# A hybrid decoder trunk on one core: residual kept with tokens on partitions, down projection as seven half-block products of sums

## The chip, the core and the metric

The kernel runs on one core of one Trainium2 chip. The core has a matrix engine (TensorE, "PE" in the profile), a vector engine (DVE), a scalar engine (ACT), GpSimd (POOL), a queue of transfers (SP) and two memories on chip, one of which (PSUM) takes the products. The metric is the device time of one execution in microseconds (us), as the median of several runs.

## The reference

Two layers, each with a token mixer of four head groups (spatial gating, retention, forgetting attention, latent attention) and a squared-ReLU channel MLP, over 512 tokens of width 1024 in float32. The parts that the change touches, cut to what matters:

```
for l in range(DEPTH):                      # DEPTH = 2
    h = rms_norm(x, g_mix_norm[l])
    y = ...four groups from h @ w_in[l], each normalised...
    x = x + y @ w_out[l]
    h = rms_norm(x, g_ffn_norm[l])
    x = x + square(relu(h @ w_up[l])) @ w_down[l]     # D_FF = 4096
return rms_norm(x, g_final)
```

## The kernel before

**Products.** Each float32 operand is split into a rounded high part and a low remainder. A product of 128 rows is three matrix instructions (`three`: high by high, high by low, low by high), so that a product over 1024 rows by 512 columns is 24 of them. A unit of weights (`Unit`, 128 x 1024, 0.5 MB) is fetched by SP into a tile `raw`; ACT casts it into `wh`, DVE subtracts into `wl`.

**Residual.** `xT` holds x with the features on partitions: 8 tiles of 128 features by 512 tokens. In the output projection and in the MLP the weights are the operand that is loaded into the matrix engine, and 512 tokens stream past them (`feat_tile`). Each result of 128 x 512 is added to its tile of `xT` by DVE. `Norm.feed` then scales it by the gain, splits it, squares it on ACT and sums the squares over the eight tiles on POOL and DVE. `tok_rsqrt` sums over partitions with a matrix of ones (`onesr`), and `bcast_tok` brings the factor 1/rms back to all partitions, again with products by ones.

**MLP.** D_FF is taken in four quarters of 1024. For each quarter eight up tiles are made (each from its own unit of weights), evacuated by DVE (ReLU times the factor `rbc`), squared on ACT and split; then eight down tiles of 24 instructions each are added to `xT`. The last quarter of the last layer makes its down tiles for 256 tokens at a time, and normalises and stores one half while the other is computed.

**Order.** All instructions are recorded with what they read and write. A list scheduler (`_Order.schedule`) then writes a fixed order for each engine, from costs and latencies in a table, with the numbers of buffers as limits: `u` (128 x 512, 46 buffers), `wh` and `wl` (6 each), `raw` (3), `quad` (3), and the eight banks of PSUM in tags `acc` 2, `s` 3, `t` 2, `pv` 1. On the chip each engine works through its order and waits where an operand is not there. All engine instructions are issued from one line of the recorder, L202, so rows of the profile are told apart by tile names, out<-in, the input that streams first and the one that is loaded second.

Of the kernel before, what the change touches and what calls it, by code (L numbers as in the profile page):

```python
# [11 lines left out]
F32 = mybir.dt.float32  # L12
# [21 lines left out]
NU = 46  # L34
NW = 6

# per-layer parameter columns
# [7 lines left out]
# shape-only constant columns  # L45
# [8 lines left out]
class _Tile:  # L54
    """A tile of a pool, taken from it when its first writer is emitted."""

    def __init__(self, od, pool, tag, bufs, shape, dtype, psum):
        self.pool, self.tag, self.bufs, self.shape, self.dtype, self.psum = pool, tag, bufs, shape, dtype, psum
        self.name = f"{tag}_{len(od.tiles)}"
        self.real = None  # L60
        self.left = 0
        self.seq = od.tag_n.setdefault(tag, [0, bufs, []])
        self.no = len(self.seq[2])
        self.seq[2].append(self)
        self.writes, self.reads = [], []
        self.held = False
        od.tiles.append(self)
# [11 lines left out]
class _View:  # L79
    """A part of a tile: the steps that lead to it, and what it covers."""  # L80
# [78 lines left out]
class _Op:  # L159
    __slots__ = ("eng", "call", "cost", "lat", "succ", "npred", "ready", "tiles", "news", "prio", "no", "start", "unit", "alt", "table")  # L160


class _Order:
    """Records the kernel's instructions with what they read and write, then issues them in the order of a list
    scheduling: per engine the most urgent instruction whose operands and buffers should be there by then."""
# [40 lines left out]
    def cost(self, eng, fn, out, ins, k):  # L206
        n = int(np.prod(out.shape[1:])) if isinstance(out, _View) else 0
        ps = any(v.tile.psum for v in ins)
        if eng == "pe":
# [6 lines left out]
            return max(n / 2.4 + 2.5, 105.0 if a.dtype == BF16 else 110.0)  # L216
# [15 lines left out]
    def record(self, eng, fn, args, kw):  # L232
# [31 lines left out]
        o.tiles, o.news = [], []  # L264
        for v, wr in [(x, False) for x in ins] + [(x, True) for x in outs]:
# [8 lines left out]
            if t not in o.tiles:  # L274
                o.tiles.append(t)
                t.left += 1
                if not t.writes:
                    o.news.append(t)
# [12 lines left out]
    def schedule(self):  # L291
# [22 lines left out]
        while ev:  # L314
# [9 lines left out]
            for o in cand[e]:  # L324
# [8 lines left out]
                for x in o.news:  # L333
# [24 lines left out]
            for x in o.news:  # L358
# [40 lines left out]
RESERVE = {"u": 10}  # L399
# [4 lines left out]
def hybrid_kernel(ctx: ExitStack, tc: tile.TileContext, xT_d, par_d, sgu_d, con_d, con2_d, wg2_d, win_d, wmla_d, wout_d, wup_d, wdn_d, out_d):  # L404
# [22 lines left out]

    def quad():
# [5 lines left out]
    class prio:  # L434
        """urgency of what is recorded inside: its place in the program, moved forward by `ahead`"""
# [20 lines left out]
    # ---------------------------------------------------------------- tensor engine  # L456
    def mm(out, a, b, start, stop):
        PE.matmul(out, a, b, start=start, stop=stop)
# [4 lines left out]
    def three(ps, ah, al, bh, bl, first, last):  # L463
        mm(ps, ah, bh, first, False)
        mm(ps, ah, bl, False, False)
        mm(ps, al, bh, False, last)

    # ---------------------------------------------------------------- weights
# [8 lines left out]
    class Unit:  # L477
        def __init__(self, src, n=1024, nsplit=None, spare=False, first=None):
# [4 lines left out]
            self.raw = mk(wpool, "raw", 3, (P, 1024))  # L483
            for c in ((0, n),) if first is None else ((0, first), (first, n)):
                Q.dma_start(self.raw[:, c[0]:c[1]], src[:, c[0]:c[1]])
            self.spare = spare
            if spare:
                self.h, self.l = (u(F32R), u(F32R)), (u(F32R), u(F32R))
                for i in range(2):
                    split(self.h[i], self.l[i], self.raw[:, i * T:(i + 1) * T])  # L490
            else:
                self.h = mk(wpool, "wh", NW, (P, 1024), F32R)
                self.l = mk(wpool, "wl", NW, (P, 1024), F32R)
                for c in ((0, k),) if first is None else ((0, first), (first, k)):
                    cs = slice(*c)
                    (od.copy if first else S.copy)(self.h[:, cs], self.raw[:, cs])
                    V.tensor_tensor(self.l[:, cs], self.raw[:, cs], self.h[:, cs].bitcast(F32), op=ALU.subtract)
            od.unit = None

        def part(self, t, k):  # L500
            return t[k // 4][:, chunk(k % 4)] if self.spare else t[:, chunk(k)]

        def hi(self, k):
            return self.part(self.h, k)

        def lo(self, k):
            return self.part(self.l, k)
# [14 lines left out]
    # ---------------------------------------------------------------- constants  # L522
    xT = cst("xT", (P, KD, T))
    par = cst("par", (P, DEPTH * NPV + KD))
# [4 lines left out]
    Q.dma_start(xT[:, 0], xT_d[:, 0])  # L529
    g2w = [Unit(wg2_d[0, 0], 2 * NG2, first=NG2)]  # L530
    Q.dma_start(xT[:, 1], xT_d[:, 1])
    Q.dma_start(xT[:, 2:4], xT_d[:, 2:4])
    g2w += weights(lambda i: wg2_d[0, i + 1], 1, 2 * NG2)
    Q.dma_start(xT[:, 4:6], xT_d[:, 4:6])
    g2w += weights(lambda i: wg2_d[0, i + 2], 1, 2 * NG2)
    Q.dma_start(xT[:, 6:8], xT_d[:, 6:8])
# [22 lines left out]
    # while the first operands are on their way: the scalar engine's table, and the tensor engine's clock  # L559
# [7 lines left out]
    # ---------------------------------------------------------------- helpers  # L567
# [6 lines left out]
    def split_gain(src, g):  # L574
        h, lo = u(F32R), u(F32R)
# [4 lines left out]
    def tok_rsqrt(acc, n, eps):  # L580
        """per-token (n**-1 * sum_p acc[p, tok] + eps) ** -0.5, tokens on partitions"""
# [13 lines left out]
    def bcast_tok(r):  # L595
        """r[tok, c] -> PSUM [any partition, tok]"""
# [13 lines left out]
    class Norm:  # L610
        """split of x * gain, and the root mean square of x per token"""

        def __init__(self, g, sq_eng=None):
            self.g, self.sq_eng = g, sq_eng
# [3 lines left out]
        def feed(self, k, split=True):  # L618
            xk = xT[:, k]
            if split:  # L620
                self.h[k], self.l[k] = split_gain(xk, self.g[:, k:k + 1])
# [4 lines left out]
            if self.sq_eng is None:  # L626
                S.activation(sq, xk, AF.Square)
            else:
                self.sq_eng.tensor_tensor(sq, xk, xk, op=ALU.mult)
# [3 lines left out]
        def finish(self, bc=True):  # L633
            self.r = tok_rsqrt(self.acc, DM, EPS)
            pb = bcast_tok(self.r)
            if bc:
                self.rbc = u()
                V.tensor_copy(self.rbc, pb)
            else:
                self.rbc = pb  # L640

    def tok_group(us, ncols, nrm, evac, banks):
        """z[tok, ncols] = sum_k, chunks in sets of len(banks)"""
# [14 lines left out]
    def feat_tile(w, ks, evac, m, o0=0, bank="acc"):  # L658
        """output tile of 128 features; ks: hi/lo operand tiles"""
# [42 lines left out]
        # group norm, features on partitions  # L702
# [13 lines left out]
    def tok_to_feat(yt, grp):  # L716
        """yt[c]: [P, 256] token-major, already normalised -> two hi/lo feature tiles with the gain"""
# [8 lines left out]
    def std_heads(src, dst, eps):  # L726
        """dst = standardised src over each head's 64 columns"""
# [491 lines left out]
```

## Time and profile before

| | |
|---|---|
| runs | 1192.19, 1196.79 and 1196.87 us, median 1196.79 |
| profiled execution, first to last instruction | 1192.4 us (the page gives no time for what lies around it) |
| PE busy | 1171.5 us, 98% of the span |
| weight loads into PE | 966.1 us, 81% |
| DVE busy | 685.2 us, 57% |
| ACT busy | 504.8 us, 42% |
| POOL busy | 91.9 us, 8% |
| read from memory | 103.44 MB |

Busy time of an engine is an average over stages: the mixers (about 0 to 245 us and 600 to 830 us) and the MLPs (the rest) have different limits. The chain of waits, followed back from the last instruction, tells which engine sets the end in a stretch.

### The profile page before, as it was taken

What the parts mean: (1) busy time and instruction counts of PE and PEld (TensorE: products, weight loads), DVE (VectorE), ACT (ScalarE), POOL (GpSimd) and SP (SyncE); (2) the same over time, 40 slices, a digit from 0 to 9 for tenths busy, and PEclk for the clock granted to TensorE, in tenths of its full rate; (3) what the DMA queues carried; (4) which work ended last, traced back from release to release, by engine and by line L of the source; (5) the groups of instructions that cost most, each with busy time, mean ns of one, the idle gap of its engine ahead of it and who ended that gap; (6) DMA issues with size and microseconds to landing.
All of it is one profiled execution on the core that took longest, in us unless ns stands there. A gap on an engine that the chain in (4) does not pass through costs nothing.

```text
span 1192.4 us, 14647 instructions
## 1 busy us (share of the span) xinstructions
PE 1171.5 (98%) x5662; PEld 966.1 (81%) x5662; DVE 685.2 (57%) x1299; ACT 504.8 (42%) x865; POOL 91.9 (8%) x100
## 2 busy tenths in 40 slices
PE   8999999999999999999999999999999999999997
PEld 7768788878888888888886778887888888888897
DVE  7985778774344344345469667789643534443533
ACT  6975445444133233134358473455431422322432
POOL 4200012120000000000240000212000000000000
PEclk9999999999999999999999999999999999999999
DMA  7322022223322323232221122132223232323202
GB/s 257 97 71 71 29 96 81 97 71 106 97 98 94 101 92 103 91 104 83 99 84 59 53 67 76 36 124 89 89 89 105 88 107 88 106 88 106 88 19 71
DMA packets 31941, 106.48 MB, mean 89 GB/s; under 512 B 3712, under 2 KB 6400, under 8 KB 31872
## 3 DMA queue, kind: packets, MB, share of 16 engines
q1 hardware_dynamic: 31872, 105.55, 26.8%
q8 instruction: 44, 0.72, 0.3%
q14 instruction: 25, 0.20, 0.1%
HBM read 103.44 MB, written 2.10 MB: 89 GB/s over the span
## 4 chain that ended last, share of the span: by engine, by line
PE 87%; DVE 6%; issue 3%; ACT 2%; DMA 1%; POOL 0%; SPq 0%; POOLq 0%; DVEq 0%; ACTq 0%
PE acc L202 48%; PE s L202 34%; DVE u L202 3%; PE t L202 3%; PE pv L202 2%; ACT u L202 2%; DVE wl L202 1%; DVE xT L202 1%; DMA raw<-win 1%; ACT wh L202 1%; DMA xT<-xT 1%; DVE sm L202 0%; POOL sm L202 0%; SPq L202 0%; DVE state L202 0%
## 5 line engine op out<-in xcount | busy, mean ns | idle before, releaser
L202 PE MATMUL acc<-u,wh 128*128 128x512 f32 (+1 forms) x1376 | 420.6, 385 | 6.9 <-DVE u L202 5.5
L202 ACT CAST wh<-raw 128x1024 fp32r<-128x1024 f32 (+2 forms) x190 | 197.3, 1039 | 519.6 <-PE acc L202 255.8
L202 PE MATMUL s<-u,wh 128*128 128x512 f32 (+1 forms) x1160 | 346.3, 381 | 0.0
L202 PEld LDWEIGHTS acc<-u,wh 128*128 128x128 f32 x1376 | 255.5, 189 | 59.0 <-DVE u L202 6.1
L202 PE MATMUL acc<-u,wl 128*128 128x512 f32 (+1 forms) x688 | 264.8, 385 | 0.0
L202 DVE TENSOR_TENSOR wl<-raw,wh 128x1024 fp32r<-128x1024 f32 (+3 forms) x191 | 231.7, 1214 | 55.2 <-ACT wh L202 54.5
L202 PEld LDWEIGHTS s<-u,wh 128*128 128x128 f32 x1160 | 215.0, 188 | 41.7
L202 PE MATMUL s<-u,wl 128*128 128x512 f32 (+1 forms) x580 | 220.6, 380 | 0.0
L202 PE MATMUL acc<-wh,u 128*128 128x512 f32 (+2 forms) x576 | 169.2, 367 | 0.7 <-ACT wh L202 0.6
L202 PEld LDWEIGHTS acc<-u,wl 128*128 128x128 f32 x688 | 129.7, 189 | 25.6 <-issue 1.1
L202 PEld LDWEIGHTS s<-u,wl 128*128 128x128 f32 x580 | 109.1, 188 | 20.7
L202 PEld LDWEIGHTS acc<-wh,u 128*128 128x128 f32 x576 | 104.3, 189 | 17.8 <-issue 2.0
L202 PE MATMUL acc<-wl,u 128*128 128x512 f32 (+2 forms) x288 | 106.3, 369 | 0.6 <-DVE wl L202 0.6
L202 DVE TENSOR_TENSOR xT<-acc,xT 128x512 f32<-128x512 f32 (+1 forms) x68 | 44.5, 656 | 99.9 <-PE acc L202 99.7
L202 DVE TENSOR_TENSOR u<-u,u 128x512 fp32r<-128x512 f32 (+4 forms) x146 | 94.7, 652 | 11.9 <-ACT u L202 10.9
L202 POOL TENSOR_TENSOR sm<-sm,mhalf 128x4 f32<-128x4 f32 (+3 forms) x38 | 39.5, 1042 | 718.7 <-DVE sm L202 689.6
L202 DVE TENSOR_TENSOR xT<-s,xT 128x512 f32<-128x512 f32 (+1 forms) x52 | 33.7, 648 | 103.6 <-PE s L202 103.5
L202 ACT ACTIVATE u<-u 128x512 f32<-128x512 f32 (+1 forms) x120 | 65.6, 548 | 37.5 <-DVE u L202 36.9
L202 ACT CAST u<-u 128x512 fp32r<-128x512 f32 (+3 forms) x120 | 73.4, 620 | 14.1 <-DVE u L202 11.4
L202 DVE SCALAR_TENSOR_TENSOR u<-acc,u 128x512 f32<-128x512 f32 x36 | 24.8, 690 | 81.8 <-PE acc L202 81.8
L202 DVE SCALAR_TENSOR_TENSOR u<-s,u 128x512 f32<-128x512 f32 x32 | 22.1, 690 | 78.2 <-PE s L202 78.2
L202 POOL TENSOR_TENSOR u<-u,u 128x512 f32<-128x512 f32 x20 | 33.6, 1679 | 373.2 <-ACT u L202 372.5
(111 smaller groups left out, 907.3 us busy)
## 6 DMA issues: line engine op xcount, KB each, us to landing
raw<-wup SPq DMA_DIRECT2D x64, 512.0 KB, 3.3
raw<-wdn SPq DMA_DIRECT2D x64, 512.0 KB, 3.3
raw<-win SPq DMA_DIRECT2D x36, 512.0 KB, 3.4
raw<-wout SPq DMA_DIRECT2D x16, 512.0 KB, 3.3
raw<-wg SPq DMA_DIRECT2D x7, 420.0 KB, 3.2
raw<-wmla SPq DMA_DIRECT2D x4, 512.0 KB, 3.4
xT<-xT SPq DMA_DIRECT2D x3, 512.0 KB, 7.4
outT<-xT SPq DMA_DIRECT2D x6, 256.0 KB, 2.2
```

Source lines behind the costliest of these rows:

```text
L202: getattr(e, fn)(*[g(a) for a in args], **{n: g(a) for n, a in kw.items()})
```

## The change

Four things change together.

**The residual is kept as `xt`, tokens on partitions** (4 tiles of 128 tokens by 1024 features). In the output projection the activations are loaded and 512 columns of weights stream (`out_group`); the result is added to half a tile of `xt`. The mean of squares is accumulated by ACT along the row while it squares (`TokNorm.feed`). For the next products the residual is turned to features on partitions by 32 transposes of 128 x 128 on PE, eight tiles of four, each then scaled and split (`TokNorm.turn`). The factor of the MLP's norm is not applied to the up tiles: its square (`r2`) multiplies the down products when they are added, since ReLU and square let a positive factor through. The last norm needs no products: each token's factor is on its partition.

**The down product of a quarter** (512 tokens x 1024 by 1024 x 1024) is taken as a product of 2 x 2 blocks in the seven-product form: sums and differences of blocks are formed on DVE, four of the activations and four of the weights, then seven products of half blocks (two token tiles, 512 rows, 512 columns: 24 matrix instructions each) are made, and several results are accumulated on in one bank and read by DVE in between (14 additions to `xt` in place of 8). The blocks `2` and `3` of the weights are fetched twice, so a quarter fetches 12 units for its down products in place of 8.

**Alternation.** The up tiles of the next quarter alternate with the seven products: up tile, product, up tile, and so on. The first quarter's eight up tiles stand alone, and so do the last quarter's seven products. ReLU is one instruction on DVE or ACT, the squares are two of 256 columns on either.

**Pools.** `u` 46 to 37 buffers, `wh`/`wl` 6 to 5; `raw` goes, and 10 tiles `big` of 128 x 1024 take fetched weights, the first input, and some tiles of the mixers that lay in `u`. The cost table's figure for a matrix instruction and the limits for reserved buffers change with it.

The diff, cut to its core:

```diff
-NU = 46
-NW = 6
+NU = 37
+NW = 5
+NBIG = 10
...
+    class TokNorm:
...
+        def feed(self, c, hf):
+            S.activation(u(), x2(c, hf), AF.Square, scale=DM ** -0.5, accum_out=self.ss[:, 2 * c + hf:2 * c + hf + 1])
+
+        def turn(self, hf):
+            for k in range(4 * hf, 4 * hf + 4):
+                tp = psum("t")
+                for c in range(NCH):
+                    tr(tp[:, chunk(c)], xt[:, c, k * P:(k + 1) * P])
+                self.h[k], self.l[k] = split_gain(tp, self.g[:, k:k + 1])
...
-        for un in range(4):
-            w = Unit(wout_d[l, un])
-            for i in range(2):
-                feat_tile(w, yD + yC, add, un * 2 + i, i * 512)
...
-        nrm.finish()
...
+        def out_group(units, ks, last=False):
+            for hf in range(2):
+                us = [Unit(wout_d[l, un]) for un in units[hf]]
+                for c in range(NCH):
+                    ps = psum(rot[nout[0] % 5])
...
+                    V.tensor_tensor(x2(c, hf), ps, x2(c, hf), op=ALU.add)
+                    if last:
+                        nrm.feed(c, hf)
+                if last:
+                    nrm.turn(hf)
+
+        out_group([[0, 1], [2, 3]], yD + yC)
+        out_group([[4], [5]], yBT)
+        out_group([[6], [7]], yAT, True)
+        nrm.square()
...
-            def evac_up(t, ps):
-                a = u()
-                V.scalar_tensor_tensor(a, ps, 0.0, nrm.rbc, op0=ALU.max, op1=ALU.mult)
-                S.activation(a, a, AF.Square)
-                hi, lo = u(F32R), u(F32R)
-                split(hi, lo, a)
...
-            for t in range(QBLK):
-                feat_tile(Unit(wup_d[l, qf * QBLK + t]), kin, evac_up, t, bank=rot[t % 5])
...
-            for m in range(KD):
-                feat_tile(Unit(wdn_d[l, qf * KD + m]), act, evac_dn, m, bank=rot[m % 5])
...
+            def product(x, raws, bank, first, done):
+                xs = []
+                for g in range(2):
+                    h, lo = u(F32R), u(F32R)
+                    split(h, lo, X[x, g])
+                    xs.append((h, lo))
+                ws = [Unit(None, raw=raws[g]) for g in range(2)]
+                for p in range(2):
+                    ps = bank(p)
+                    for g in range(2):
+                        for jj in range(2):
+                            o = jj * 256 + p * P
+                            w, cs = ws[g], slice(jj * T, (jj + 1) * T)
+                            with using(w):
+                                three(ps, xs[g][0][:, o:o + P], xs[g][1][:, o:o + P], w.h[:, cs], w.l[:, cs],
+                                      first and g == 0 and jj == 0, g == 1 and jj == 1, skip_group_check=True)
+                    done(p, ps)
...
+            def add(c, hf, ps, done=False):
+                V.scalar_tensor_tensor(x2(c, hf), ps, nrm.r2[:, c:c + 1], x2(c, hf), op0=ALU.mult, op1=ALU.add)
...
+            def p6():
+                fetch(1, 3)
+                for g in range(2):
+                    X["S3", g] = u()
+                diff(Xv("S3"), Xv("11"), Xv("21"))
+                diff(Rv(1), Rv(1), Rv(0))
+                diff(Rv(3), Rv(3), Rv(1))
+                diff(Xv("21"), Xv("21"), Xv("22"), ALU.add)
+                diff(Xv("11"), Xv("21"), Xv("11"))
+                product("11", R[3], bank(B, None), False, lambda p, ps: add(p + 2, 0, ps))
...
+            return [p1, p2, p6, p7, p4, p5, p3]
+
+        for part in ups(0):
+            part()
         for qf in range(nq):
+            a, b = downs(qf), ups(qf + 1) if qf + 1 < nq else []
+            for i in range(max(len(a), len(b))):
+                for part in b[i:i + 1] + a[i:i + 1]:
+                    part()
```

How the instructions stand now, at three places. First PE, in layer 0, where the output projection ends and the MLP begins. Before, the last tile of the output projection (bank `s_2506`) is followed by the first up tile (`acc_2519`, activations `u`, weights `wh_2264` and `wl_2277`):

```order
L202 MATMUL s_2506<-u_2320,wh_2212 128x512
L202 MATMUL s_2506<-u_2330,wh_2212 128x512
L202 MATMUL s_2506<-u_2320,wl_2227 128x512
L202 MATMUL s_2506<-u_2326,wh_2212 128x512
L202 MATMUL s_2506<-u_2337,wh_2212 128x512
L202 MATMUL s_2506<-u_2326,wl_2227 128x512
L202 MATMUL acc_2519<-u_2434,wh_2264 128x512
L202 MATMUL acc_2519<-u_2442,wh_2264 128x512
```

After the change (`s_2534` is the last tile of the output projection, `xt_333` the residual, `con_196` the identity, `s_2559` the first up tile):

```order
L201 MATMUL s_2534<-wh_2332,u_2322 128x512
L201 MATMUL s_2534<-wl_2339,u_2322 128x512
L201 MATMUL s_2534<-wh_2332,u_2330 128x512
L201 MATMUL t_2548<-con_196,xt_333 128x128 x3
L201 MATMUL t_2555<-con_196,xt_333 128x128 x3
L201 MATMUL s_2559<-u_2488,wh_2343 128x512
L201 MATMUL s_2559<-u_2502,wh_2343 128x512
L201 MATMUL t_2548<-con_196,xt_333 128x128
L201 MATMUL t_2555<-con_196,xt_333 128x128
L201 MATMUL s_2559<-u_2488,wl_2360 128x512
L201 MATMUL s_2559<-u_2494,wh_2343 128x512
L201 MATMUL s_2559<-u_2510,wh_2343 128x512
```

The transposes stand between the last output tile and the first up tile, mixed with that tile's first products, which take features turned earlier.

Second DVE, in the last quarter of layer 0's MLP. Before, between two additions to `xT` there are a subtraction for a unit of weights (`wl`) and the split for the next norm:

```order
L202 TENSOR_TENSOR xT_80<-acc_4546,xT_80 128x512
L202 TENSOR_TENSOR wl_4594<-raw_4491,wh_4582 128x1024
L202 SCALAR_TENSOR_TENSOR u_4603<-xT_80,par_72,u_4591 128x512
L202 TENSOR_TENSOR xT_80<-s_4584,xT_80 128x512
L202 TENSOR_TENSOR wl_4632<-raw_4529,wh_4620 128x1024
L202 SCALAR_TENSOR_TENSOR u_4641<-xT_80,par_72,u_4629 128x512
```

After (`acc_4789` holds the first product's results; the `u` rows are sums, differences and splits of the activations, one square among them):

```order
L201 TENSOR_TENSOR u_4192<-u_4195,u_4192 128x512
L201 TENSOR_TENSOR u_4795<-u_4767,u_4781 128x512
L201 TENSOR_TENSOR u_4704<-u_4792 128x256
L201 TENSOR_TENSOR u_4805<-u_4192,u_4798 128x512
L201 TENSOR_TENSOR u_4367<-u_4367,u_4706 128x512
L201 TENSOR_TENSOR u_4817<-u_4775,u_4786 128x512
L201 SCALAR_TENSOR_TENSOR xt_333<-acc_4789,sm_601_2595,xt_333 128x512
L201 TENSOR_TENSOR u_4827<-u_4704,u_4815 128x512
L201 TENSOR_TENSOR u_4365<-u_4367,u_4365 128x512
L201 TENSOR_TENSOR wl_4839<-big_4475,wh_4808 128x1024
L201 SCALAR_TENSOR_TENSOR xt_333<-acc_4819,sm_601_2595,xt_333 128x512
L201 TENSOR_TENSOR wl_4857<-big_4503,wh_4834 128x1024
```

There are more rows between two additions, and those for later products stand ahead of additions of earlier ones.

Third PE, in layer 0's latent attention (logits `s`, transposes `t`, sums `pv`). Before, single products of the input projection (`acc_555`) stand among its small products:

```order
L202 MATMUL s_806<-u_519,u_635 128x256
L202 MATMUL acc_555<-u_150,wh_350 128x512
L202 MATMUL t_812<-con_193,u_749 128x128 x4
L202 MATMUL t_822<-con_193,u_765 128x128
L202 MATMUL acc_555<-u_160,wh_350 128x512
L202 MATMUL acc_555<-u_150,wl_371 128x512
L202 MATMUL s_829<-u_519,u_635 128x384
```

After, the same stretch holds the attention's own rows alone:

```order
L201 MATMUL s_772<-u_545,u_599 128x256
L201 MATMUL t_778<-con_196,u_715 128x128 x4
L201 MATMUL t_788<-con_196,u_728 128x128
L201 MATMUL s_793<-u_545,u_599 128x384
L201 MATMUL pv_759<-quad_752,u_635 64x512
L201 MATMUL pv_759<-quad_693,u_635 64x384
```

The products of the input projection follow behind it.

## Rows read from the trace of the kernel before

**Rows 1.** The page: its head, busy time by engine, granted clock in 40 slices.
```profile
span 1192.4 us, 14647 instructions
PE 1171.5 (98%) x5662; PEld 966.1 (81%) x5662; DVE 685.2 (57%) x1299; ACT 504.8 (42%) x865; POOL 91.9 (8%) x100
PEclk9999999999999999999999999999999999999999
```
**Rows 2.** Five stretches: us, busy by engine (instructions), granted clock, DMA share, GB/s.
```profile
0.00:30.00 30.00, 25.21 (x109) 21.35 (x109) 21.75 (x34) 18.72 (x29) 13.45 (x19) 1.00 0.76 258
30.00:60.00 30.00, 29.22 (x135) 21.87 (x136) 28.24 (x81) 28.66 (x61) 8.62 (x14) 1.00 0.31 93
240.00:270.00 30.00, 27.25 (x113) 21.82 (x112) 22.55 (x36) 12.77 (x19) 6.31 (x4) 0.94 0.26 84
330.00:360.00 30.00, 30.00 (x134) 24.82 (x134) 13.44 (x16) 10.05 (x14) 0.00 (x0) 1.00 0.28 90
810.00:840.00 30.00, 27.25 (x120) 21.91 (x119) 25.55 (x31) 14.99 (x22) 8.87 (x5) 1.00 0.27 89
```
**Rows 3.** Chain that ended last, pieces in order of time: start, us, what.
```profile
178.05 0.22 PE t L202 x2
...
185.39 25.44 PE acc L202 x112
...
264.02 10.88 PE s L202 x48
...
1150.33 2.88 PE acc L202 x24
```
**Rows 4.** Around the start of layer 0's MLP, instructions in order of time.
```profile
245.90 2.04 POOL L202 TENSOR_TENSOR u<-u,u 128x512 f32<-128x512 f32 x1 [2.57 <-ACT u L202]
...
246.74 2.42 DVE L202 SCALAR_TENSOR_TENSOR u<-xT,par,u 128x512 fp32r<-128x512 f32 x2
...
248.55 0.79 PE L202 MATMUL acc<-u,wh 128*128 128x512 f32 x1 [2.75 <-DVE u L202]
...
250.42 0.63 PE L202 MATMUL acc<-u,wl 128*128 128x512 f32 x1
...
250.84 0.63 PE L202 MATMUL acc<-u,wh 128*128 128x512 f32 x1
```
**Rows 5.** The same place in steps of 2 us (columns as in rows 2).
```profile
246.00:248.00 2.00, 0.00 (x0) 0.00 (x0) 2.00 (x2) 2.00 (x4) 1.94 (x1) 1.00 0.09 23
248.00:250.00 2.00, 1.45 (x4) 1.17 (x5) 2.00 (x4) 0.02 (x1) 0.00 (x0) 0.60 0.75 240
250.00:252.00 2.00, 2.00 (x7) 1.57 (x6) 1.02 (x2) 0.00 (x0) 0.00 (x0) 0.55 0.00 0
```
**Rows 6.** The end of the kernel, in order of time.
```profile
1180.76 2.56 PE L202 MATMUL acc<-u,u 128*128 128x256 f32 x20
...
1185.17 0.70 POOL L202 TENSOR_TENSOR sm<-sm,mhalf 128x2 f32<-128x2 f32 x1 [23.49 <-DVE sm L202]
...
1187.15 2.46 SPq L202 DMA_DIRECT2D outT<-xT  x5
```
**Rows 7.** Groups by form: operation, out<-in, count | busy, mean ns | idle before, releaser.
```profile
L202 PE MATMUL t<-con,u 128*128 128x128 f32 x240 | 41.3, 276 | 0.7 <-DVE u L202 0.3 <-ACT u L202 0.2
...
L202 DVE TENSOR_TENSOR wl<-raw,wh 128x1024 fp32r<-128x1024 f32 x180 | 220.9, 1228 | 54.8 <-ACT wh L202 54.2
L202 DVE TENSOR_TENSOR u<-u,u 128x512 fp32r<-128x512 f32 x80 | 54.7, 690 | 2.7 <-ACT u L202 2.6
...
L202 DVE SCALAR_TENSOR_TENSOR u<-t,par,u 128x512 fp32r<-128x512 f32 x14 | 9.9, 746 | 3.2 <-ACT u L202 3.1
...
L202 DVE TENSOR_TENSOR u<-u,u 128x256 f32<-128x256 f32 x20 | 8.5, 424 | 6.1 <-ACT u L202 5.9
...
L202 DVE COPY quad<-t 128x512 f32<-128x512 f32 x12 | 8.2, 685 | 2.7 <-PE t L202 2.7
```
**Rows 8.** ACT's groups by form.
```profile
L202 ACT CAST wh<-raw 128x1024 fp32r<-128x1024 f32 x180 | 189.3, 1053 | 501.6 <-PE acc L202 249.3 <-PE s L202 231.9 <-issue 10.7
...
L202 ACT CAST u<-u 128x512 fp32r<-128x512 f32 x80 | 49.1, 620 | 9.4 <-DVE u L202 7.4
```
**Rows 9.** Who waited for whom: us in total, times, longest.
```profile
DVE wl L202 <- ACT wh L202: 54.5, 129, 11.4
```

More of the change, by code (lines that the diff above doesn't have):

```diff
@@ L454, in hybrid_kernel, with mm, three @@
     od.record = record
-    def mm(out, a, b, start, stop):
-        PE.matmul(out, a, b, start=start, stop=stop)
+    def mm(out, a, b, start, stop, **kw):
+        PE.matmul(out, a, b, start=start, stop=stop, **kw)
     def tr(out, a):
         PE.transpose(out, a, ident)
[L463 to L466, printed above, removed]
+    def three(ps, ah, al, bh, bl, first, last, **kw):
+        mm(ps, ah, bh, first, False, **kw)
+        mm(ps, ah, bl, False, False, **kw)
+        mm(ps, al, bh, False, last, **kw)
     chunk = lambda c: slice(c * P, (c + 1) * P)
@@ L477, in hybrid_kernel, with __init__ @@
     class Unit:
-        def __init__(self, src, n=1024, nsplit=None, spare=False, first=None):
+        def __init__(self, src, n=1024, nsplit=None, first=None, raw=None):
             k = nsplit or n
@@ L482, in __init__, with load @@
             od.unit = self.no
[L483 to L488, printed above, removed]
-                for i in range(2):
[L490 to L497, printed above, removed]
-            od.unit = None
[L500 to L507, printed above, removed]
+            self.raw = raw
+            if raw is None:
+                self.raw = load(src, n, first)
+            self.h = mk(wpool, "wh", NW, (P, 1024), F32R)
+            self.l = mk(wpool, "wl", NW, (P, 1024), F32R)
+            for c in ((0, k),) if first is None else ((0, first), (first, k)):
+                cs = slice(*c)
+                (od.copy if first else S.copy)(self.h[:, cs], self.raw[:, cs])
+                V.tensor_tensor(self.l[:, cs], self.raw[:, cs], self.h[:, cs].bitcast(F32), op=ALU.subtract)
+            od.unit = None
+    def load(src, n=1024, first=None, tile=None):
+        raw = big() if tile is None else tile
+        for c in ((0, n),) if first is None else ((0, first), (first, n)):
+            Q.dma_start(raw[:, c[0]:c[1]], src[:, c[0]:c[1]])
+        return raw
     def weights(ref, n, size=1024):
@@ new lines, in hybrid_kernel, with ups, part, evac @@
+        if fin:
+            gf = load(gf_d)
+        quarters = [{} for _ in range(nq)]
+        def ups(qf):
+            X = quarters[qf]
+            def part(t):
+                kk, g, jj = t // 4, t // 2 % 2, t % 2
+                def evac(m, ps):
+                    a = u()
+                    od.either(("act", "activation", (a, ps, AF.Relu), {}), ("dve", "tensor_scalar", (a, ps, 0.0, None), {"op0": ALU.max}))
+                    for hf in range(2):
+                        key = f"{hf + 1}{kk + 1}", g
+                        if not jj:
+                            X[key] = u()
+                        dst, a2 = X[key][:, jj * 256:jj * 256 + 256], a[:, hf * 256:hf * 256 + 256]
+                        od.either(("act", "activation", (dst, a2, AF.Square), {}), ("dve", "tensor_tensor", (dst, a2, a2), {"op": ALU.mult}))
+                feat_tile(Unit(wup_d[l, qf * QBLK + t]), kin, evac, t, bank=rot2[t % 4])
+            return [lambda t=t: part(t) for t in range(QBLK)]
@@ L1216 @@
     r = run_bass_kernel_spmd(nc, [arrays], core_ids=[0])
-    o = r.results[0]["outT"]
-    return np.ascontiguousarray(o.transpose(1, 0, 2).reshape(DM, T).T)[None]
+    o = r.results[0]["out"]
+    return np.ascontiguousarray(o.transpose(1, 0, 2).reshape(T, DM))[None]
```

254 lines of the change are left out of this document (136 added, 118 removed).

## The prediction

> **What bounds the kernel now.** I read the page's busy shares first: PE 98%, DVE 57%, ACT 42% [rows 1]. A busy PE says little alone, so I took the stretches next. Within the MLP, 330 to 360 us, PE is busy 30.00 of 30 us, DVE 13.44 and ACT 10.05, at the full clock [rows 2], and the chain of waits is PE alone: 48 products of 512 columns in 10.88 us, or 0.2267 us each [rows 3]. So there a matrix instruction is worth 0.2267 us and DVE's work nothing, as long as it fits. It holds in a stretch of the mixer too, where products of both orientations come (also those that load activations and stream weights, as all down products now will): 112 in 25.44 us [rows 3]. Products of 256 columns cost 0.12 us (24 in 2.88) [rows 3].
>
> Elsewhere PE waits. From 0 to 60 us it is idle for 4.79 + 0.78 us; in 30 to 60 us DVE is busy 28.24 and ACT 28.66 of 30 us, so the attention there goes at their pace [rows 2]. At the start of either layer's MLP it is idle for 2.75 us (27.25 busy of 30, twice) [rows 2]: it waits for a split by DVE, which ran two such instructions in 2.42 us while POOL summed squares for 2.04 us [rows 4], against 0.746 us for one alone [rows 7]. In layer 0 the clock then fell: 0.60 and 0.55 in the next 4 us [rows 5], that is, to its 1.2 GHz level for most of it; products started 0.42 us apart (250.42, 250.84) [rows 4]. Lost: 2 x 0.40 + 2 x 0.45 = 1.7 us.
>
> **Removed.** (a) A quarter's down product takes 7 x 24 = 168 products of 512 columns in place of 192; eight quarters now take 1344, which is what seven took. The 384 products of 256 columns of the last one go: 384 x 0.12 = **46.1 us**. (b) The two MLP norms no longer sum and broadcast by products with ones (four each), the second layer's first norm no longer sums by them (two): 10 x 0.2267 = **2.3 us**. (c) The two waits and the slow clock at the MLP's start, 2.75 x 2 + 1.7 = 7.2 us. The squares are now summed along the row by ACT, so POOL no longer runs beside the splits. The last output tile's addition (0.7 us) and the transposes behind it lie beside the first up tile's twelve products over features turned earlier (2.7 us), as the order shows; the remaining four pairs arrive at DVE's 0.75 us each, PE wants one per 0.68. I leave 0.5 us each: **6.2 us** gained. Without that cover the old 7.2 would stay. (d) The end. Before, 1183.3 (end of the last main products) to 1192.4 is 9.1 us, with an addition, small products by ones, POOL's 0.70 and a broadcast by products, then five multiplications and stores [rows 6]. After: one addition and two multiplications (0.746 each, by the row nearest in form), a square (0.62 as a cast [rows 8]), POOL 0.70, the last store's way, of which 2.46 us of issuing is the nearest row, and half a dozen hand-overs of about 0.2. I put 7.5: **1.6 us** gained.
>
> **Added on PE.** (e) 96 transposes (three norms of 32). In the chain two take 0.22 us [rows 3], so 0.11 each: **10.6 us**. Their own duration is 276 ns [rows 7], but they overlap. The Trainium skill ("TensorE: Matmul & The Clock Gate", Part 4: PE-mode transpose) gives about 275 ns for a transpose in a kernel's context; charged in full, that would be 26.4 us in place of 10.6. The row has the same duration, the chain of waits a spacing of less than half of it. (f) In the mixers, twelve products of 0.2267 us that lay inside the two latent attentions now stand behind them (I counted the interleaved products in both orders: 17 before, 5 after). If the attention goes at DVE's pace, they cost their time: 2.7, put at **3 us**. Fewer buffers can only add; no row prices it. Bounds: nothing, and as much idle time again as the first 60 us have, in both layers, 11 us. I take the low end since the small products keep their order and DVE's work there is the same.
>
> **Added on DVE and ACT.** A quarter of the MLP, with rows 7: 22 weight subtractions (8 up, 14 down) x 1.228 = 27.0; 8 block differences of weights x 1.228 = 9.8; 14 splits and 8 sums of activations x 0.690 = 15.2; 14 additions with a factor x 0.746 = 10.4; 8 ReLUs from PSUM x 0.685 (the copy's) = 5.5; some 7 of the 16 squares x 0.424 = 3.0. Sum 70.9 us. Before it was 16 x 1.228 + 24 x 0.69 = 36.2. PE has 192 + 168 = 360 products, 81.6 us, against 87.0 before. ACT: 22 x 1.053 + 14 x 0.620 = 31.8, and some 9 squares at 0.6 at most, 37 [rows 8]. So DVE is at 87% of PE's time, no longer at 42%, and in single pairs of an up tile and a product (10.9 us of PE) the order gives it 9 to 11.3 us. Transfers: 12 + 8 units of 0.5 MB per 81.6 us is 129 GB/s; the first 30 us ran at 258 [rows 2], so they stay hidden. If DVE is late, next late are a bank of tag `t`, which an up tile and both halves of a product share, and the additions that a bank's next product waits for.
>
> (g) The stalls. Interleaved part, six quarters: between nothing and DVE's pace plus waits (rival A); I take 0.5 us a quarter, **3 us**. The last quarter's seven products stand alone: PE 168 x 0.2267 = 38.1 us, DVE 14 x 1.228 + 8 x 1.228 + 22 x 0.69 + 14 x 0.746 = 52.6, short by 14.5. But the order puts the weight differences and first splits ahead. From the ReLU of the last but one up tile to the last subtraction, DVE's rows are 13 + 1 of 1.228, 22 of 0.690, 12 of 0.746, one of 0.685 and two of 0.424: 42.9 us, and PE has 188 products and 16 transposes up to where it needs that subtraction: 42.6 + 1.8 = 44.4. It fits with 1.5 us to spare, DVE never idle. In layer 0 the transposes stand right behind additions for which DVE is then behind by one to two us: I take 3 us in layer 0, 1 in layer 1, **4 us**; bounds nothing and 14.5 each.
>
> **Sum**, against the profiled span: 1192.4 − 46.1 − 2.3 − 6.2 − 1.6 + 10.6 + 3 + 3 + 4 = 1156.8. The span lies 4.4 us under the median of the runs and level with the lowest; I add a third of that: **1158 us**, 3.2% faster. A difference of 0.5% (6 us) is about what a measurement of this kernel tells from none.
>
> **Rivals.**
> *A: DVE paces the MLP.* Against: 70.9 of 81.6 us. For: DVE works in a fixed order, and 129 times it waited for ACT's cast ahead of a subtraction, 0.42 us in the mean [rows 9]; a quarter now has 36 such pairs. If each cost that, 15.2 us: 86.1 a quarter, 4.5 over PE; eight of them, 36 us in place of the 3: 1191. Half of it: 1174.
> *B: the last products go at DVE's pace*, as if nothing was done ahead: 29 us in place of 4: 1183. Against it stands the order; for it, that the sums above hold no wait.
> *C: slower than before, by the clock.* The engine's clock fell after a wait of 2.75 us in layer 0 and products came 0.42 us apart, 0.2 more than at full clock [rows 4, 5]. If the last products stall often enough to hold it at 1.2 GHz, 336 products in both layers x 0.2 = 67 us: 1225. It decides from about 200 products at the low level. Against: the same 2.75 us in layer 1 left the clock at 1.00, and so did 4.79 us of idle scraps in the first 30 us [rows 2].
> *D: the mixers pay for the pools*: 11 to 15 us in place of 3: 1168. For: attention loses its fill, and `u` shrinks by nine.
> *E: a transpose takes its whole duration on PE*, 96 x 0.165 = 16 us more than in (e), by the row of 276 ns [rows 7]: 1174. The spacing of 0.11 us speaks against it [rows 3]. It is what the page of the Trainium skill named above would give.
>
> **Numbers.** Forecast 0.58, with its own range 1146 to 1170; A 0.14, half of it with the full price; B 0.09; C 0.06; D 0.08; E 0.02; no case (less than 1146) 0.03. The range 1145 to 1185 holds the forecast, half of A, B, D and E, and leaves out C, the full A and the tail below: about 0.16. Faster by over 0.5% (under 1190.8): all but C, the full A and a little: 0.87; within 0.5%: the full A, 0.06; slower 0.07.
>
> **What would show it.** Right: in the MLP the chain of waits is PE at 10.88 us per 48 products, PE busy full in a stretch like 330 to 360, DVE 25 to 27 of 30 us; 96 transposes at 0.11 us; no wait at the MLPs' starts and no POOL sums there; the mixers' length within 4 us of before; the last 45 us of each MLP with DVE full and PE idle under 4 us. Wrong: DVE full and PE waiting for `wl` or splits in the middle quarters (A), idle time of over 5 us in the last seven products (B) or a clock near 0.5 there (C), or a first output projection that starts over 8 us later (D).

## The result, and the profile after

| kernel | median (us) | runs | ratio to before, 95% interval |
|---|---|---|---|
| before | 1196.73 | 1192.19 to 1196.87 | |
| after | 1154.12 | 1153.47 to 1155.71 | 0.966 [0.9641, 0.9679] |

The change made the kernel 3.4% faster. The forecast was 1158 us, in a range of 1145 to 1185.

The page of the kernel after, head and busy time by engine, against [rows 1]:

```profile
span 1152.6 us, 14443 instructions
PE 1132.4 (98%) x5340; PEld 923.5 (80%) x5340; DVE 897.4 (78%) x1574; ACT 549.2 (48%) x963; POOL 61.6 (5%) x85
```

PE has lost 39.1 us of busy time and the span 39.8: PE is as full as before, with less to do. DVE has gained 212 us, and the end pays nothing for it.

The stretches, columns as in [rows 2]:

```profile
0.00:30.00 30.00, 26.04 (x109) 21.81 (x109) 21.90 (x34) 19.09 (x30) 16.72 (x27) 1.00 0.93 338
30.00:60.00 30.00, 29.10 (x137) 21.46 (x137) 25.58 (x81) 23.56 (x56) 2.49 (x3) 1.00 0.39 133
60.00:90.00 30.00, 27.89 (x131) 18.04 (x130) 25.91 (x76) 17.70 (x43) 2.95 (x5) 1.00 0.06 21
...
240.00:270.00 30.00, 30.00 (x150) 24.92 (x149) 21.13 (x29) 15.30 (x30) 0.00 (x0) 1.00 0.26 79
330.00:360.00 30.00, 30.00 (x134) 24.86 (x133) 23.05 (x30) 13.02 (x17) 0.00 (x0) 1.00 0.42 137
...
600.00:630.00 30.00, 28.52 (x136) 20.70 (x135) 24.85 (x70) 23.34 (x52) 2.11 (x2) 1.00 0.32 106
630.00:660.00 30.00, 26.19 (x125) 17.64 (x124) 24.66 (x68) 18.82 (x43) 1.48 (x2) 1.00 0.06 17
810.00:840.00 30.00, 30.00 (x147) 24.87 (x146) 19.44 (x28) 14.77 (x28) 0.00 (x0) 1.00 0.27 83
```

In the MLP PE is full with DVE at 23.05 of 30 us. At the start of both MLPs (240 to 270, 810 to 840) the 2.75 us of idle time are gone, and the clock is at its full level. In the mixers PE is idle for longer than before: in the attention of layer 0 (60 to 90 us, 2.11) and of layer 1 (600 to 660, 5.29). The same stretches of the kernel before:

```profile
60.00:90.00 30.00, 30.00 (x149) 20.84 (x148) 24.20 (x74) 21.47 (x53) 1.01 (x1) 1.00 0.21 72
...
600.00:630.00 30.00, 29.28 (x146) 25.11 (x145) 21.01 (x65) 15.98 (x35) 12.29 (x18) 1.00 0.23 72
630.00:660.00 30.00, 29.21 (x144) 19.82 (x142) 27.35 (x83) 27.33 (x66) 0.00 (x0) 1.00 0.20 64
```

The chain of waits in the last part of layer 0's MLP, where its last products stand alone, and at the end of layer 1's; pieces as in [rows 3]:

```profile
548.39 5.44 PE acc L201 x24
553.83 10.88 PE s L201 x48
564.71 0.65 PE t L201 x6
...
1134.14 10.89 PE acc L201 x48
1145.04 0.03 issue
1145.06 2.07 DVE xt L201 x3
```

The chain is PE alone, product behind product at 0.2267 us, into the last quarter and up to its last product. The transposes stand in it at 0.11 us (six in 0.65). Around the start of layer 0's MLP, in order of time, against [rows 4]:

```profile
247.19 0.82 PE L201 MATMUL t<-con,xt 128*128 128x128 f32 x6
247.77 0.71 PE L201 MATMUL s<-u,wh 128*128 128x512 f32 x2
248.31 0.38 PE L201 MATMUL t<-con,xt 128*128 128x128 f32 x2
```

The first up product follows the transposes with no idle time noted. The length of the stages follows. An MLP is counted from its first up product to the end of its last down product, a mixer from there to the next MLP's first up product. In the kernel before, that product stands right behind the last output tile and starts at 241.73 us, and 16 products of its tile run before the wait of [rows 4]; in layer 1 it starts at 826.84.

| stage | before (us) | after (us) | difference |
|---|---|---|---|
| up to layer 0's first up product | 241.7 | 247.8 | +6.0 |
| MLP of layer 0 | 354.0 | 329.7 | −24.3 |
| mixer of layer 1 | 231.1 | 239.7 | +8.6 |
| MLP of layer 1 | 356.5 | 327.9 | −28.6 |
| tail | 9.1 | 7.6 | −1.5 |

### The profile page after: what moved, and what is told of

Read it like the earlier page. It is cut to its first block, busy times and chain, and to the rows that moved or that the text cites. A ratio compares the mean times of both kernels' runs of the same rounds, so it can differ in the third digit from the quotient of the medians.

```text
span 1152.6 us, 14443 instructions
## 1 busy us (share of the span) xinstructions
PE 1132.4 (98%) x5340; PEld 923.5 (80%) x5340; DVE 897.4 (78%) x1574; ACT 549.2 (48%) x963; POOL 61.6 (5%) x85
## 4 chain that ended last, share of the span: by engine, by line
PE 93%; DVE 4%; ACT 2%; issue 1%; DMA 0%; POOL 0%; SPq 0%; DVEq 0%; POOLq 0%; ACTq 0%
PE acc L201 35%; PE s L201 25%; PE t L201 23%; PE pv L201 10%; DVE u L201 2%; ACT u L201 1%; DVE wl L201 1%; DMA big<-xT 0%; DVE big L201 0%; DVE quad L201 0%; DVE xt L201 0%; ACT wh L201 0%; ACT quad L201 0%; POOL sm L201 0%; SPq L201 0%
## 5 line engine op out<-in xcount | busy, mean ns | idle before, releaser
L201 ACT CAST wh<-big 128x1024 fp32r<-128x1024 f32 (+2 forms) x224 | 233.1, 1041 | 356.2 <-PE t L201 106.4
L201 PE MATMUL acc<-wh,u 128*128 128x512 f32 (+2 forms) x1200 | 371.6, 381 | 0.3 <-ACT wh L201 0.2
L201 DVE TENSOR_TENSOR wl<-big,wh 128x1024 fp32r<-128x1024 f32 (+2 forms) x225 | 271.8, 1211 | 52.4 <-ACT wh L201 51.6
L201 PEld LDWEIGHTS acc<-wh,u 128*128 128x128 f32 x1200 | 220.5, 189 | 39.2 <-ACT wh L201 0.5
L201 PE MATMUL acc<-wl,u 128*128 128x512 f32 (+2 forms) x600 | 227.3, 379 | 2.0 <-DVE wl L201 2.0
L201 PE MATMUL t<-u,wh 128*128 128x512 f32 x512 | 157.6, 389 | 0.0
L201 PE MATMUL s<-wh,u 128*128 128x512 f32 (+1 forms) x464 | 148.8, 384 | 0.0
L201 PEld LDWEIGHTS acc<-wl,u 128*128 128x128 f32 x600 | 113.3, 189 | 21.4 <-DVE wl L201 2.6
L201 PE MATMUL t<-u,wl 128*128 128x512 f32 x256 | 99.6, 389 | 0.0
L201 PEld LDWEIGHTS s<-u,wh 128*128 128x128 f32 x256 | 47.8, 188 | 9.7
```

Source lines behind the costliest of these rows:

```text
L201: getattr(e, fn)(*[g(a) for a in args], **{n: g(a) for n, a in kw.items()})
```

## The experiments

All are edits of the kernel after, `b1_nopool` of the kernel before. The kernels of a batch (the first four, the next four, the last two) ran on one chip each, beside the kernel before with 1195.78, 1195.18 and 1193.55 us. The kernel after ran beside it at 1196.73, so its differences to these runs are differences between chips too, and by the times alone one of under 3 us cannot be told from nothing.

| run | edit | median (us) | ratio to before |
|---|---|---|---|
| e1_eight | eight plain half-block products | 1197.95 | 1.0017 [1.0003, 1.0030] |
| e2_apart | no alternation | 1156.38 | 0.9671 [0.9651, 0.9692] |
| e3_up2 | up subtractions twice | 1155.37 | 0.9663 [0.9642, 0.9683] |
| e3_down2 | down subtractions twice | 1186.08 | 0.9917 [0.9890, 0.9944] |
| e4_turn2 | transposes twice | 1164.52 | 0.9757 [0.9734, 0.9781] |
| e5_res8 | 8 of `u` held back | 1148.24 | 0.9617 [0.9597, 0.9638] |
| e6_apart_down2 | no alternation, down subtractions twice | 1227.61 | 1.0279 [1.0258, 1.0299] |
| b1_nopool | before, no POOL sums | 1186.07 | 0.9927 [0.9903, 0.9951] |
| e7_factor | factor on the up tiles | 1155.29 | 0.9678 [0.9656, 0.9699] |
| e8_res8_nopool | e5_res8, no POOL sums | 1146.20 | 0.9599 [0.9576, 0.9622] |

**Where the gain is: `e1_eight`.** Layout, alternation and pools stay; the seven products with sums become eight plain ones.

```diff
-            return [p1, p2, p6, p7, p4, p5, p3]
+            for n in range(2):
...
+                for kk in (1, 2):
+                    for hf in (1, 2):
...
+                                product(f"{hf}{kk}", R[b], bank(banks[hf], "acc" if hf == 1 else "s"), kk == 1,
+                                        last if kk == 1 else lambda p, ps: add(p + 2 * hf - 2, n, ps, True), hold[kk])
...
+            return parts
```

> The same frame (residual with tokens on partitions, alternation, pools), but the down product of a quarter is taken as eight plain half-block products, 192 matrix instructions in place of 168, without sums of blocks. Theory (the number of instructions on TensorE decides): 8 quarters x 24 x 0.2267 = 43.5 us more than after the change, 1198 us (1193 to 1203), with DVE's load in the MLP down to about 45 us a quarter. Rival (a good part of the gain comes from the token layout and the alternation, through fewer waits): the time stays under 1180.

Measured: 1197.95 us, 43.8 more than after. 192 more products of 512 columns at 0.2267 us are 43.5. The gain is the number of PE's instructions; all else in the change together comes out about even with the kernel before (2.2 us more beside it). Even does not mean nothing: gains and losses of several us cancel there, as the part on the prediction shows.

**What alternation is worth: `e2_apart`.**

```diff
-            for i in range(max(len(a), len(b))):
-                for part in b[i:i + 1] + a[i:i + 1]:
-                    part()
+            for part in downs(qf) + (ups(qf + 1) if qf + 1 < nq else []):
+                part()
```

> Only the alternation is undone: a quarter's seven products are written before the next quarter's eight up tiles. DVE then has 52.6 us of work beside 38.1 us of products in every quarter, not only in the last. Theory (the order lets DVE work ahead during the up tiles, as it does in the last quarter): 1154 to 1166 us. Rival (the alternation is what hides DVE): 14.5 us more in each of six quarters, up to 1241.

Measured: 1156.38, 2.3 us more. PE is busy 30.00 of 30 us in every stretch from 240 to 600 us and from 810 to 1140, also where DVE has the most to do:

```profile
300.00:330.00 30.00, 30.00 (x134) 24.86 (x133) 28.00 (x35) 15.73 (x20) 0.00 (x0) 1.00 0.56 176
```

So the planner moves DVE's work for the products ahead under the up tiles by itself, and the 2.3 us do not lie in the MLPs.

**How much room DVE has: `e3_up2`, `e3_down2`.** The subtraction that makes `wl` is made twice, for the up units (`twice` is theirs) or for the down units (the condition is then `raw is not None`); the second writes the same values.

```diff
-                V.tensor_tensor(self.l[:, cs], self.raw[:, cs], self.h[:, cs].bitcast(F32), op=ALU.subtract)
+                for _ in range(2 if twice else 1):
+                    V.tensor_tensor(self.l[:, cs], self.raw[:, cs], self.h[:, cs].bitcast(F32), op=ALU.subtract)
```

> Each weight subtraction of an up tile is done twice on DVE (the second writes the same values): 64 x 1.228 = 79 us more work, 9.8 a quarter. Theory (DVE costs nothing until it has no idle time left): from the first down product to the end of an MLP, DVE has then some 296 us of work where TensorE has 283, so 5 to 13 us per layer: 1164 to 1180 us. Rival 1 (DVE's work is on the path already): all of it, 1233. Rival 2 (DVE has ample room): 1154 to 1157.

> Each weight subtraction of a down product is done twice on DVE: 112 x 1.228 = 137.5 us more, 17.2 a quarter. Theory: DVE has 332 to 335 us of work from the first down product to the end of an MLP where TensorE has 283, so it sets the pace: 43 to 50 us more per layer, 1240 to 1254 us. Rival 1 (all of it on the path): 1292. Rival 2 (ample room): under 1180.

Measured: 1155.37 and 1186.08 us. My size of the room was wrong in both: the up subtractions cost 1.2 us where I had expected at least 10, the down ones 32 where I had expected 86. Busy times over layer 0's MLP, first the kernel after, then `e3_up2`, then `e3_down2`:

```profile
240.00:570.00 330.00, 330.00 (x1482) 273.50 (x1481) 264.76 (x335) 143.20 (x211) 1.56 (x3) 1.00 0.36 114
```
```profile
240.00:570.00 330.00, 330.00 (x1479) 272.98 (x1477) 295.79 (x360) 145.10 (x214) 1.57 (x3) 1.00 0.36 116
```
```profile
240.00:570.00 330.00, 324.36 (x1431) 266.70 (x1429) 304.08 (x355) 142.15 (x211) 0.00 (x0) 0.99 0.35 113
```

DVE is busy 264.76 of 330 us, 80%, and not the 87% of the prediction; 65 us are free. The chain of `e3_down2` shows why:

```profile
541.05 2.40 DVE u L201 x4
543.45 4.54 DVE wl L201 x4
548.00 0.66 DVE xt L201
```

Back to back, a subtraction of weights takes 1.135 us of DVE's time, a split 0.60, an addition 0.66: each some 0.09 less than its own duration in [rows 7], since one instruction starts before the last has ended. I had added durations: 81 instructions a quarter x 0.09 = 7.3, so 63.6 and not 70.9 of 81.6 us, 78%. In the kernel after, DVE is busy 63.91 and 65.25 us in two such stretches (300 to 381.6 and 381.6 to 463.2 us). The 32 up subtractions of a layer are then 36.3 us and fit into 65; the 56 of the down units are 63.6 and nearly fill it. In `e3_down2` DVE falls behind towards the end of the MLP, where nothing is left to work ahead under:

```profile
510.00:540.00 30.00, 30.00 (x134) 24.86 (x133) 30.00 (x35) 14.11 (x23) 0.00 (x0) 1.00 0.29 89
540.00:570.00 30.00, 24.36 (x93) 18.42 (x92) 27.87 (x32) 13.20 (x19) 0.00 (x0) 0.89 0.30 94
570.00:600.00 30.00, 25.53 (x118) 21.21 (x117) 27.42 (x39) 15.10 (x28) 4.07 (x8) 0.83 0.09 33
```

That is 10.1 us of idle PE, and products at the low clock behind it (granted 0.89 and 0.83), of the 17.2 us by which layer 0's MLP ends later than in the kernel after (594.66 in place of 577.43).

**Alternation once DVE is nearly full: `e6_apart_down2`**, both edits above together.

> The changed kernel without the alternation of up tiles and products, and with the subtraction for each down weight unit made twice (112 more of 1.23 us, 137.5 us of DVE). With alternation the same extra work gave 1186; without it and without the extra work 1156. Theory 1 (the planner works ahead across parts anyway; the room is DVE's idle time, about 65 us in each MLP): 1183 to 1192. Theory 2 (alternation is what gives DVE its room; without it seven products of 38 us stand against 70 us of DVE's work, and buffers end the work-ahead): over 1200.

Measured: 1227.61, 41.5 us more than `e3_down2`. PE waited 39.0 us for `wl`, ten times. Theory 2's time holds: without the alternation work is moved ahead only so far. Whether buffers end it, as the theory says, or how far ahead the planner looks, was not tried. In the kernel after as it is this does not decide (2.3 us); it gives the reserve.

**What a transpose costs: `e4_turn2`.**

```diff
-                for c in range(NCH):
+                for c in range(2 * NCH):
+                    c = c % NCH
                     tr(tp[:, chunk(c)], xt[:, c, k * P:(k + 1) * P])
```

> The changed kernel (1154.1 us), with each of the 96 transposes that turn the residual made twice into the same bank: 96 more instructions on PE, nothing else. The theory (a transpose costs its spacing in the chain, 0.11 us, because its 276 ns overlap with its neighbours): 96 x 0.11 = 10.6, so 1163 to 1167. The rival (it costs its whole duration): 96 x 0.276 = 26.5, so 1178 to 1183. If the transposes lie in waits that are there anyway, under 1159.

Measured: 1164.52, 10.4 us more for 96 transposes (9.8 by the spans of the profiled executions, 1162.4 and 1152.6): 0.10 to 0.11 each, the spacing, though in the kernel after they have a mean duration of 272 ns:

```profile
L201 PE MATMUL t<-con,xt 128*128 128x128 f32 x96 | 14.4, 272 | 0.0
```

**What the mixers lost: `e5_res8`.**

```diff
-RESERVE = {"u": 16, "quad": 3, "big": 12}
+RESERVE = {"u": 8, "quad": 3, "big": 12}
```

> The changed kernel with one number of the planner changed: it holds back 8 buffers of u for earlier steps in place of 16. By its order 62 and 60 products of 24-product input tiles then stand ahead of the first products with the values in the latent attention, in layer 0 and 1, where the changed kernel has 48 and 48 and the kernel before 57 and 56. The theory on the mixers (they are 7.5 us longer since the attention lost its fill, of which some 5 us is PE idle): the 12 to 14 products at 0.2267 us come back into the attention's waits in both layers, 2 to 3 us each, so 1148 to 1151, with PE idle by 1 us or less in 60 to 90 us in place of 2.1. The rival (attention goes at DVE's pace whatever stands between): within 1.5 us of 1154.

Measured: 1148.24, 5.9 us less than after. Its stretches at the two attentions:

```profile
60.00:90.00 30.00, 30.00 (x149) 20.87 (x148) 25.95 (x77) 24.01 (x59) 1.01 (x1) 1.00 0.10 31
630.00:660.00 30.00, 30.00 (x144) 20.90 (x143) 25.37 (x68) 21.87 (x48) 1.01 (x1) 1.00 0.11 36
```

PE is full in both. The input projection's products are back between the attention's small ones. It was not the number of `u` buffers (37 in both) that had put them behind, but how many of them the planner keeps for earlier steps: 16 in the kernel after, where the kernel before held back 10 of 46. By the stages of the table above the loss is larger than the 7.5 us that I expected to explain: the mixers are 14.6 us longer after the change (I had taken the last product ahead of the wait for the MLP's first), and `e5_res8` takes 6.6 of them back (244.8 and 236.1 us).

**Why PE waited at the MLP's start: `b1_nopool`**, in the kernel before:

```diff
-                (G if k < KD - 2 else V).tensor_tensor(self.acc, self.acc, sq, op=ALU.add)
+                V.tensor_tensor(self.acc, self.acc, sq, op=ALU.add)
```

> The kernel before (1196.8 us), with the sums of squares of its norms all on DVE in place of POOL for six of eight. The theory on the boundary (a POOL sum beside it stretches a DVE split from 0.75 to 1.21 us, and PE waits 2.75 us in each layer's start of the MLP, with the low clock behind it in layer 0): splits at 0.75 us again, but eight sums of 0.69 us more on DVE, so a wait of 1 to 3 us each and 1191 to 1197. The rival (the wait is the last output tile's addition and the splits behind it, whoever sums): within 1 us of 1196.8, the splits at 0.75 us and the wait still 2.5 us or more.

Measured: 1186.07, 9.1 us less than the kernel before beside it, more than either theory gave. The splits by form, first in the kernel before, then in `b1_nopool`, and the latter's starts of the MLPs:

```profile
L202 DVE SCALAR_TENSOR_TENSOR u<-xT,par,u 128x512 fp32r<-128x512 f32 x32 | 34.3, 1085 | 2.5 <-ACT u L202 2.4
```
```profile
L202 DVE SCALAR_TENSOR_TENSOR u<-xT,par,u 128x512 fp32r<-128x512 f32 x32 | 23.9, 746 | 2.0 <-ACT u L202 1.8
```
```profile
240.00:270.00 30.00, 30.00 (x134) 24.82 (x133) 23.59 (x41) 15.28 (x24) 1.01 (x1) 1.00 0.32 105
...
810.00:840.00 30.00, 30.00 (x134) 24.82 (x133) 26.59 (x47) 16.17 (x24) 1.01 (x1) 1.00 0.28 92
```

The trace of the kernel before tells the same within itself: its 20 splits that overlap a POOL sum take 1289 ns in the mean, up to 1800, the other 12 take 744. Up to the end of layer 0's wait four splits and one subtraction of weights beside POOL took 4.0 us longer than their like elsewhere, and the wait is 2.75. In `b1_nopool` DVE does more sums there and is done sooner: the last of the eight splits ends at 248.01 us in place of 250.42.

No wait is left at either start, where I had left 1 to 3 us. Part of that is another order: the planner now mixes the second up tile's products in after 18 of the first, where before 22 stood together, and puts one subtraction of weights behind the splits. How much of the gain is the order and how much the shorter splits was not separated. By the two profiled executions (1192.4 and 1183.9 us) the gain is 8.5 us, and 8.2 of it lie in the MLPs: layer 0's is 4.9 us shorter, layer 1's 3.3. The idle time of 2.75 in each and the 1.7 of the low clock make 7.2 of that; the rest is products that stood further apart behind the waits (the first two in layer 1 started 0.34 us apart, 833.66 and 834.00, at the full clock). The mixers are as long as before (241.5 for 241.7 and 231.0 for 231.1 us).

**The norm's factor: `e7_factor`.**

```diff
-        nrm.square()
+        nrm.finish()
...
-                    od.either(("act", "activation", (a, ps, AF.Relu), {}), ("dve", "tensor_scalar", (a, ps, 0.0, None), {"op0": ALU.max}))
+                    V.scalar_tensor_tensor(a, ps, 0.0, nrm.rbc, op0=ALU.max, op1=ALU.mult)
```

> The changed kernel (1154.1 us) with the MLP norm's factor applied as before the change: 1/rms is brought to all partitions by products with ones, DVE multiplies by it as it does the ReLU of each up tile, and the down products are added without a factor. Added on PE: the broadcast's few products in each layer, 1 to 2 us in all; on DVE the 64 ReLUs with the factor at 0.75 us, some of which ACT took. Theory (DVE has some 65 us of idle time in each MLP, and the first up tile waits for little): 1154 to 1158. The rival (the factor hangs on the last square, so up tiles' banks are held and PE waits at the MLP's start): 2 to 4 us for each layer on top, 1159 to 1164.

Measured: 1155.29, 1.2 us more, which cannot be told from nothing between two chips. The page counts four more matrix instructions (5344 for 5340), 0.9 us at 0.2267, and PE is busy 30.00 of 30 us at both MLPs' starts as in the kernel after. Moving the factor behind the down product is worth about that and no more.

**The two finds together: `e8_res8_nopool`**, `e5_res8` with the edit of `b1_nopool` in the one norm that still sums by POOL.

> The kernel with 8 buffers of u held back (1148.2 us), and the sums of squares of the first norm, the one that is still summed by POOL, all on DVE. The theory (a POOL sum stretches a DVE split beside it): PE's idle time in the first 30 us shrinks by 0.4 us as it did in the kernel before, so 1147 to 1148.5. The rival (the first 30 us wait for transfers and splits whoever sums): no difference that can be told, 1148 to 1150.

Measured: 1146.20 (1145.6 to 1146.3), the fastest of all, 4% below the kernel before. It is 2.0 us less than `e5_res8`, but on another chip, and the two ratios to the kernel before (0.9599 [0.9576, 0.9622] and 0.9617 [0.9597, 0.9638]) do not tell them apart. The traces do for the first 30 us: PE is busy 26.46 against 25.43 in `e5_res8`, the splits take 747 ns in place of 1104, and the attention's first sums of values start at 63.53 in place of 65.16 us. That is 1.0 us more of PE's work in that stretch, more than the theory's 0.4.

## Why the prediction was right

**What bounds the kernel.** In the MLP a matrix instruction was said to be worth 0.2267 us and DVE's work nothing as long as it fits. `e1_eight` shows the first (43.8 us for 192), `e3_up2` the second (1.2 us for 64 more subtractions). Not every sign came as written: DVE is busy 23.05 of 30 us in 330 to 360, not 25 to 27, and the mixers are 6.0 and 8.6 us longer, not within 4.

**(a), (b)** The 384 products of 256 columns at 0.12 us are 46.1; no run puts them back, and the same arithmetic as 192 products of 512 measured 43.8. The stretch that held them took 47.4 us (1135.77 to 1183.16), since the small products of the last norm's first half stood among them: 1.3 us more that went, which the sum had left out. The ten ones-products were not measured apart.

**(c)** I left 0.5 us at each MLP's start; none is there. The wait is gone, and by the lengths of the MLPs in `b1_nopool` that is worth 8.2 us and not 6.2. The cause that the prediction named, POOL beside the splits, is borne out by the splits' durations and by `b1_nopool`, there together with a new order. The sentence that without the cover of the first up tile's products the old 7.2 would stay is not: the kernel before has such a cover, 16 products over features split earlier, and waited all the same. Whether the transposes of the kernel after would stall without theirs was not tried.

**(d)** 7.5 us of tail predicted, 7.6 measured. **(e)** 10.6 predicted, 10.4 measured by doubling.

**(f)** The term that was too small: 3 us, against some 9. The mixers are 14.6 us longer by the table of stages. 58 of the 96 transposes stand in them (22 and 36), 6.3 us at 0.108, and two products by ones are gone from them, 0.5; 8.8 us are left. Of these 4.7 show as PE's idle time (12.64 us in the mixers after, 7.92 before), the rest, then, lies in products further apart; `e5_res8` takes 6.6 us of the length and 5.1 of the idle time back. The mechanism was the named one, the attention without its fill. What failed is the count of twelve products at their own time: up to the start of the second sums with the values the orders have 65 and 61 products of the input projection ahead before, and 48 and 48 after, which is 30 fewer; up to the end of these sums they have 78 and 76 against 48 and 48, which is 58 fewer. What fewer buffers cost by themselves stays open: with the same 37, half the reserve gives the fill back.

**(g)** The term that was too large: 7 us, measured nothing. The chain shows no stall in the interleaved quarters nor among the last products. The step that failed is the sum of DVE's durations. A quarter's 70.9 us are 63.6 back to back, and the 42.9 us that had to fit into 44.4 before the last subtraction are, for 51 instructions at 0.09 less, 38.3. The 0.5 us for each interleaved quarter was an allowance with no row behind it.

With 1.3 and 2.0 us less from (a) and (c), 5.8 more from (f) and 7 less from (g), 1156.8 becomes 1152.3, against a span of 1152.6. That the total came so near is in part luck: the two large errors, 5.8 and 7 us, have opposite signs.

**Rivals.** A (DVE paces the MLP): no; in the kernel after DVE still waited 36 times for ACT's cast, 51.6 us in all, but it has 65 us to spare in a layer, and PE is never idle in layer 0's MLP. B (last products at DVE's pace): no; they follow each other at 0.2267 us. C (clock): no; the granted clock is 1.00 in every stretch of both MLPs. But its mechanism is real where DVE is late. In `e6_apart_down2` a wait of 5.16 us was followed by products 0.43 us apart, at a granted clock of 0.64 from 318.8 to 324.0 us, so at the 1.2 GHz level for most of it:

```profile
318.80 1.22 PE L201 MATMUL acc<-wl,u 128*128 128x512 f32 x2 [5.16 <-DVE wl L201]
319.82 1.05 PE L201 MATMUL s<-wh,u 128*128 128x512 f32 x2
320.68 0.63 PE L201 MATMUL s<-wl,u 128*128 128x512 f32 x1
321.10 1.05 PE L201 MATMUL s<-wh,u 128*128 128x512 f32 x2
```

D (the mixers pay): in kind yes, at some 9 us, nearer to its 11 to 15 than to the 3 of the sum, and by the reserve more than by the shrunken pool. E (whole duration of a transpose): no, by `e4_turn2`.

## What to carry to other kernels

Where PE is full, count its instructions, and price them and those of the engine beside it by their spacing back to back in a chain, not by the duration of one: that decided 7 us here on DVE and 16 on PE. After a change of buffers and layout, look for PE idle in the stages that were not the aim: one number of the planner cost 5.9 us, 14% of the whole gain. Measure a stage from the same instruction in both kernels: a start taken at a wait, 16 products into the MLP, hid half of what the mixers grew by here. And undo a suspected contention in the old kernel before crediting the new one: 9.1 us of what a rewrite seemed to need were one word, with the order that followed from it.

## What the runs showed of the hardware

A POOL addition of two tiles in on-chip memory stretched the DVE split beside it: in the kernel before, 20 splits that overlap one took 1289 ns in the mean and up to 1800, 12 others 744. Six sums were dearer on the idle engine than on the busy one. Four DVE additions of a product from PSUM to `xT`, each wholly beside a POOL sum, took 676 to 692 ns, as the form does elsewhere (687): with one of their two inputs in PSUM they were not stretched. The Trainium skill ("SBUF — State Buffer", SBUF: two separate sides) says that DVE and GpSimd share one pair of ports under an exclusive lock, which a DVE operation with two inputs there contends for while GpSimd reads there too. The 1289 and 744 ns agree with that.

The transposes kept 272 ns each and cost some 0.108 us; PE's records of one instruction overlap with the next, and so, by 0.09 us, do DVE's.
